# A transformer-layer kernel on one core: second phi matrix and gather issued after the first, odd work tied behind a pass's splits, row copies tied to the FFN's weight slabs

## The chip, the cores and the metric

The kernel runs on one core of a Trainium2 chip. The metric is device microseconds (us) of one execution, the median of three runs. Engines in the text: PE is TensorE (matmuls; PEld is its weight load), DVE is VectorE, ACT is ScalarE, POOL is GpSimd, SP is SyncE, which issues most DMAs here. Each engine runs its instructions in the order in which they were placed on it.

## The reference

One decoder layer over 512 prompt tokens and 32 sample tokens (8 sequences of 4), width 1024, FFN width 2816, all fp32:

- `mod = silu(c) @ w_ada + b_ada` gives shifts, scales and gates; `h = rmsnorm(x, norm1) * (1 + sc1) + sh1`.
- `h @ w_in` feeds a gated width-3 convolution and a native sparse attention: compressed blocks, selected blocks, a sliding window, each with its own keys and values. The compressed keys and values are `gelu(blocks @ w_phi1 + bias) @ w_phi2`, separately for K and V; for the sample tokens the blocks come from a paged cache through a page table, and the bias is the block position embedding `pe_cmp` times `w_phi1`.
- The two mixers are merged by sigmoid gates, projected by `w_out`, and added to x.
- `x += g2 * ((silu(h2 @ w_gate) * (h2 @ w_up)) @ w_down)`, then a last RMSNorm.
- Among the outputs is `new_win_sample = concat(cache_win, new rows)[:, 4:]`: the old window shifted by four rows.

## The kernel before

**Number format.** Every fp32 operand is split into a high and a low part. `split` (line 170) does this for a 128-column piece of a weight slab: ACT copies the piece into `wh` (L176), DVE subtracts into `wl` (L177); both tags have two buffers. `mm3` makes three matmuls of each product, in this order: wh with x high (L181), wh with x low (L182), wl with x high (L183). `to_hilo` (L211 on ACT, L212 on DVE) does the same for activations. Tokens come in two halves of 288 and 256 columns. A weight slab (`slab`, L167) is one 1 MB DMA on SP into one of three `raw` buffers.

**The start.** Before the projections a loop of 16 passes, n = 0 to 15, compresses the paged cache. A pass gathers 1 MB of rows (`cmp_gather`, L428, an indirect DMA issued by POOL, two `gt` buffers), copies them into transposable form (`cmp_copy`, L436, two DVE copies), transposes them (`cmp_T`: 16 transposes on PE, L444, four to a PSUM bank; ACT makes `xh`, L446; DVE makes `xl`, L447), and multiplies by the phi matrices (`cmp_M`: 24 matmuls a pass, 12 for K and 12 for V, L458 to L460). The two phi matrices are loaded by `phi_load` (L391, 1 MB each, `rphi`, into two of the three `raw` buffers) and split in quarters by `phi_split` (L396 on ACT, L397 on DVE). The third `raw` buffer holds the rows of c, of x_sample and of the convolution state (`xs`).

Between the passes lies odd work that uses the same engines: silu of c and its transposes (L549 to L553), `phi_bias` (`pb`, L403: 32 matmuls, the last readers of `rphi`), `x_rows` (transposes of x and its squares, L512 to L520), `mod_slab` (one slab of `w_ada`, L229, 16 instructions that the trace counts in 32 pieces), `inv_from_sums` and `inv_bcast` (the inverse norms, L255 to L294), `modulate`. The first slab of w_ada goes into the buffer of the first phi matrix, so it can only be issued when the first bias group has read that.

**The FFN.** Loop c2 = 1 to 10 (line 1343) loads one slab of w_gate and one of w_up (256 columns each) and takes them in two 128-column pieces. For a piece: split of the gate piece, its matmuls for both halves with `silu` on ACT into `ffg` (L1295), split of the up piece, its matmuls for both halves, and per half a DVE product `ffg` = up x silu (L1300), then f_hi on ACT (L211) and f_lo on DVE (L212). Eight 1016 KB copies from DRAM to DRAM make the shifted rows (`win_shift`, L1336).

**What sets the order.** The program is written in the order of its calls, but the framework's scheduler, with a cost model, places the instructions on each engine; `tc.issue_after(ins)` keeps what is written under it behind `ins`. A program order on an engine is fixed once it is built: an instruction whose input is late holds all that stand behind it on its engine.

Of the kernel before, what the change touches and what calls it, by code (L numbers as in the profile page):

```python
# [19 lines left out]
KC = 8  # L20
# [79 lines left out]
def build(tc, a, o):  # L100
# [19 lines left out]
    def tp_ps(nm):  # L120
        return ps.tile([128, 512], F32, tag="g", bufs=5, name=nm)
# [194 lines left out]
    def make_A(nT, sc, A):  # L316
        dve.tensor_scalar_add(A, sc, 1.0)
        dve.tensor_mul(A, A, nT.rearrange("p (k x) -> p k x", x=1).broadcast_to([128, 8, 9]))
# [70 lines left out]
    def phi_load(v):  # L389
        rw = raw_tile("rphi").rearrange("p (k f) -> p k f", k=16)  # L390
        sync.dma_start(rw, a["w_phi1"][v].rearrange("(k p) f -> p k f", p=128))  # L391
        rws.append(rw)

    def phi_split(v, qt):
        qv = lambda t: t.rearrange("p (s c) f -> p s c f", s=2)[:, :, 2 * qt:2 * qt + 2, :]
        act.activation(qv(wph[v]), qv(rws[v]), AF.Copy)  # L396
        dve.tensor_sub(qv(wpl[v]), qv(rws[v]), qv(wph[v]).bitcast(F32))  # L397

    def phi_bias(v):
        p = tp_ps(nm("pb"))  # L400
        for k in range(16):
            j = k % 4
            pe.matmul(p[32 * j:32 * j + 32, 0:128], lhsT=peT[:, v * 16 + k:v * 16 + k + 32], rhs=rws[v][:, k, :], start=(k < 4), stop=(k >= 12))  # L403
        t = wphip.tile([128, 128], F32, tag="pbs", bufs=2, name=nm("pbs"))
        dve.tensor_copy(t, p[:, 0:128])
        q = tp_ps(nm("pbt"))
        pe.matmul(q[:, 0:1], lhsT=t, rhs=sel, start=True, stop=True)
        dve.tensor_copy(pbias[:, v:v + 1], q[:, 0:1])
# [16 lines left out]
    def cmp_gather(bp, qt):  # L425
        t = gat.tile([128, 4 * 512], F32, tag="gt", bufs=2, name=nm("gt"))
        col = bp * 4 + qt
        pool.indirect_dma_start(out=t, out_offset=None, in_=ccv, in_offset=bass.IndirectOffsetOnAxis(ap=ixc[:, col:col + 1], axis=0))  # L428
        return t
# [10 lines left out]
    def cmp_T(v, g2t):  # L440
        for lp in range(2):
            p = tp_ps(nm("xt"))
            for g in range(4):
                pe.transpose(p[:, g * 128:(g + 1) * 128], g2t[lp][:, v * 4 + g].rearrange("p l d -> p (l d)"), ident)  # L444
            xo = xhb[v][:, lp * 512:lp * 512 + 512]
            act.activation(xo, p, AF.Copy)  # L446
            dve.tensor_sub(xlb[v][:, lp * 512:lp * 512 + 512], p, xo.bitcast(F32))  # L447

    def cmp_M(v, qt, po):
        for lp in range(2):  # L450
# [23 lines left out]
                    pe.matmul(p[0:63, b2 * 256 + g * 64:b2 * 256 + g * 64 + 64], lhsT=h1[:, (g * 2 + b2) * 63:(g * 2 + b2) * 63 + 63], rhs=w2[:, 1, :], start=True, stop=True)  # L474
            evac(vext[0:63, 2 * bp:2 * bp + 2, :], p[0:63, 0:512].rearrange("p (b x) -> p b x", b=2))

    pool.memset(vext[32:64], 0.0)

    xst = ExitStack()
    xp = mkpool(xst, "xp", side="right")  # L480
    xT = xbig("xT")
# [1 line left out]
    dve.memset(ss1, 1.0)  # L483
    phi_load(0)
    gts = [cmp_gather(0, 0)]
    sync.dma_start(xr[0], a["x_prompt"][0:128, :])
    phi_load(1)
    gts.append(cmp_gather(0, 1))
    sync.dma_start(crow[0:1], a["c_prompt"])
    sync.dma_start(crow[1:9], a["c_sample"])  # L490
    sync.dma_start(perow, a["pe_cmp"].rearrange("v l d -> (v l d)").rearrange("(k p) -> k p", p=128))
    sync.dma_start(w2, a["w_phi2"].rearrange("v p d -> p v d"))
    for r0, nme, n in ((24, "b_ada", 48), (0, "norm1", 8), (8, "norm2", 8), (16, "norm_f", 8), (72, "b_conv", 8), (80, "w_conv", 24)):
        s = a[nme]
        s = s.rearrange("a b -> (a b)") if len(s.shape) == 2 else s
        sync.dma_start(vrow[r0:r0 + n, :], s.rearrange("(k p) -> k p", p=128))
    sync.dma_start(xs, a["x_sample"])
    sync.dma_start(strow, a["state_conv"])
    for j in range(1, 4):
        sync.dma_start(xr[j], a["x_prompt"][j * 128:(j + 1) * 128, :])  # L500

    dve.tensor_reduce(sel, ident.rearrange("p (a b) -> p b a", b=32)[:, 0, :], axis=AX.X, op=ALU.add)
# [18 lines left out]

    wake()
    phi_split(0, 0)
    phi_split(1, 0)
    accs = {}

    def cmp_step(bp, qt, v):
        if qt == 0:
# [6 lines left out]
    for n in range(16):  # L535
        bp, qt = n // 4, n % 4
        g2t = cmp_copy(gts[n])
        if n + 2 < 16:
            gts.append(cmp_gather((n + 2) // 4, (n + 2) % 4))
        for v in range(2):  # L540
            cmp_T(v, g2t)
            if pend is not None:
                cmp_step(*pend)
            pend = (bp, qt, v)
        if n < 3:
            for v in range(2):
                phi_split(v, n + 1)
        if n == 0:
            act.activation(crow, crow, AF.Silu)  # L549
            cp = tp_ps("cp")  # L550
            for k in range(KC):
                pe.transpose(cp[:, k * 16:k * 16 + 9], crow[:, k * 128:(k + 1) * 128], ident[64:73, 64:73])
            dve.tensor_copy(cT[:, :, 0:9], cp[:, 0:128].rearrange("p (k n) -> p k n", k=8)[:, :, 0:9])  # L553
            pp = tp_ps("pep")
            pe.transpose(pp[:, 0:32], perow, ident[0:32, 0:32])
            dve.tensor_copy(peT[:, 0:32], pp[:, 0:32])
            for v in range(2):
                phi_bias(v)
            vp = tp_ps("vp")
            pe.transpose(vp[:, 0:104], vrow, ident[0:104, 0:104])  # L560
            dve.tensor_copy(vec, vp[:, 0:104])
        if n == 1:
            p = tp_ps("stp")
            for k in range(KC):
                pe.transpose(p[:, k * 16:(k + 1) * 16], strow[:, k * 128:(k + 1) * 128], ident[32:48, 32:48])
            dve.tensor_copy(stT, p[:, 0:128].rearrange("p (k n) -> p k n", k=8))
            x_rows(4)
        if n < 8:
            mod_slab(n)
        if 2 <= n < 6:  # L570
            x_rows(n - 2)
        if n == 6:
            iv = inv_from_sums(ss1, xp)
            iv2 = xp.tile([128, 3], F32, name="iv2")
            dve.tensor_copy(iv2[:, 0:2], iv[:, 0:2])
            dve.tensor_copy(iv2[:, 2:3], iv[:, 4:5])
            invs = (inv_bcast(iv2, 0, xp), inv_bcast(iv[:, 2:4], 1, xp))
        if n == 8:
            modp.pop()()
            make_A(n1T, sc1, A1)  # L580
            mods = [modulate(xT, invs[hf], A1, sh1, hh_, hl_, hf, xp) for hf in range(2)]
        if 8 <= n < 12:
            for g_ in mods:
                for _ in range(2):
                    next(g_)
        if n == 12:
            with tc.issue_after(last_slab[0].ins):
                sync.dma_start(x_dr, xT.rearrange("p k n -> p (k n)"))
            xst.close()
# [753 lines left out]
    for c2 in range(1, FC // 2):  # L1343
        sg, su = slab(a["w_gate"], c2 * 256), slab(a["w_up"], c2 * 256)
        if c2 <= DEC_B:
            win_shift(c2 - 1)
        for cc in range(2):
            c, g_ = c2 * 2 + cc, ffg()
            for v, fn in ((sg, lambda w, hf: ffn_gate(g_, w, hf)), (su, lambda w, hf: ffn_up(c, g_, w, hf))):
                w = split(v[:, :, cc * 128:cc * 128 + 128])  # L1350
                for hf in range(2):
                    fn(w, hf)
# [104 lines left out]
```

## Time and profile before

| | |
|---|---|
| median of 3 runs | 1346.72 us (1346.35 to 1346.86) |
| the profiled execution, its own time | 1346.54 us |
| its span in the trace | 1344.5 us |
| PE busy | 1311.2 us, 98% |
| DVE, ACT busy | 654.1 us (49%), 539.4 us (40%) |
| DMA | 193.56 MB, mean 144 GB/s |

How to read it: PE is busy nearly always, so idle time of PE is what there is to win, and new idle time of PE is what there is to lose. The time of the execution is 2.0 us above the span of the trace.

### The profile page before, as it was taken

To read this page: it belongs to the slowest core of one execution; us is meant where nothing else is said; L and a number is where in the kernel's file an instruction comes from. 1 tells how busy PE (TensorE), PEld (TensorE's weight loads), DVE (VectorE), ACT (ScalarE), POOL (GpSimd) and SP (SyncE) were. 2 spreads that over 40 slices of the span, in tenths; PEclk is the share of its full clock that TensorE was granted. 3 is DMA by queue.
4 is the path that set the end of the run, shared out by engine and by line. 5 is a ranking of instruction groups with operands and counts; after the bars stand their busy time and mean duration, and the time that the engine had idled before them with its cause. 6 is when DMAs were issued, how large, how long until landed. Compare 5 with 4: busy or idle time off the path is not lost.

```text
span 1344.5 us, 25740 instructions
## 1 busy us (share of the span) xinstructions
PE 1311.2 (98%) x10884; PEld 1212.8 (90%) x10884; DVE 654.1 (49%) x1570; ACT 539.4 (40%) x1065; POOL 69.3 (5%) x123
## 2 busy tenths in 40 slices
PE   5899999999999999999999999999999999999997
PEld 4778899999999999899777777999999999999996
DVE  3458623234454554425677676667433333323335
ACT  5335423433332334324676766435323223222223
POOL 2000030000111110001000000000000000000000
PEclk7999999999999999999999999999999999999998
DMA  7877225684534562664357246531112223123221
GB/s 263 314 275 291 95 78 175 221 266 141 206 126 170 189 236 98 168 158 130 111 163 201 90 120 167 162 128 63 64 64 95 95 64 125 56 87 87 87 63 67
DMA packets 138024, 193.56 MB, mean 144 GB/s; under 512 B 4817, under 2 KB 124761, under 8 KB 132918
## 3 DMA queue, kind: packets, MB, share of 16 engines
q1 hardware_dynamic: 133302, 149.98, 36.2%
q0 software_dynamic: 4608, 41.95, 8.4%
q8 instruction: 85, 1.39, 0.4%
q14 instruction: 29, 0.24, 0.0%
HBM read 174.47 MB, written 25.76 MB: 149 GB/s over the span
## 4 chain that ended last, share of the span: by engine, by line
PE 95%; DMA 2%; DVE 1%; ACT 0%; issue 0%; SPq 0%; POOL 0%; ACTq 0%; DVEq 0%; POOLq 0%
PE lin L181 19%; PE lin L182 19%; PE lin L183 19%; PE dn L181 3%; PE dn L182 3%; PE dn L183 3%; PE acc L1143 3%; PE ptp L1149 3%; PE xt L444 2%; PE phi L460 2%; PE phi L458 2%; PE phi L459 2%; PE modp L229 2%; PE kt L860 2%; PE sp L1118 1%; DMA rphi<-in_w_phi 1%
## 5 line engine op out<-in xcount | busy, mean ns | idle before, releaser
L181 PE MATMUL lin<-h_hi,wh 128*128 128x288 f32 (+1 forms) x1648 | 478.5, 291 | 0.0
L182 PE MATMUL lin<-h_lo,wh 128*128 128x288 f32 (+1 forms) x1648 | 474.5, 288 | 0.0
L183 PE MATMUL lin<-h_hi,wl 128*128 128x288 f32 (+1 forms) x1648 | 473.1, 287 | 0.0
L181 PEld LDWEIGHTS lin<-h_hi,wh 128*128 128x128 f32 x1648 | 310.5, 188 | 9.4 <-issue 8.1
L182 PEld LDWEIGHTS lin<-h_lo,wh 128*128 128x128 f32 x1648 | 310.0, 188 | 0.5
L183 PEld LDWEIGHTS lin<-h_hi,wl 128*128 128x128 f32 x1648 | 309.4, 188 | 0.3
L177 DVE TENSOR_TENSOR wl<-raw,wh 128x1024 fp32r<-128x1024 f32 x132 | 159.1, 1206 | 238.7 <-ACT wh L176 238.4
L176 ACT ACTIVATE wh<-raw 128x1024 fp32r<-128x1024 f32 x132 | 138.2, 1047 | 301.6 <-PE lin L182 204.0
L181 PE MATMUL dn<-f_hi,wh 128*128 128x256 f32 (+1 forms) x352 | 101.9, 290 | 0.0
L182 PE MATMUL dn<-f_lo,wh 128*128 128x256 f32 (+1 forms) x352 | 101.3, 288 | 0.0
L183 PE MATMUL dn<-f_hi,wl 128*128 128x256 f32 (+1 forms) x352 | 101.0, 287 | 0.0
L1125 ACT ACTIVATE P<-P,nms 128x512 f32<-128x512 f32 (+3 forms) x128 | 70.9, 557 | 18.7 <-DVE nms L1124 17.9
L1124 DVE CUSTOM_DVE_ANT_0 P<-sp,ta 128x512 f32<-128x512 f32 (+3 forms) x128 | 57.7, 483 | 31.0 <-PE sp L1112 23.5
L183 PEld LDWEIGHTS dn<-f_hi,wl 128*128 128x128 f32 x352 | 66.3, 188 | 0.0
L181 PEld LDWEIGHTS dn<-f_hi,wh 128*128 128x128 f32 x352 | 66.2, 188 | 0.0
L182 PEld LDWEIGHTS dn<-f_lo,wh 128*128 128x128 f32 x352 | 66.1, 188 | 0.0
L458 PE MATMUL phi<-xh,wph 128*128 128x512 f32 x128 | 53.5, 418 | 0.0
L459 PE MATMUL phi<-xh,wpl 128*128 128x512 f32 x128 | 51.4, 402 | 0.0
L460 PE MATMUL phi<-xl,wph 128*128 128x512 f32 x128 | 51.2, 400 | 0.0
L447 DVE TENSOR_TENSOR xl<-xt,xh 128x512 fp32r<-128x512 f32 x64 | 41.7, 687 | 19.0 <-ACT xh L446 19.0
L444 PE MATMUL xt<-ident,gt 128*128 128x128 f32 x256 | 36.6, 292 | 13.7 <-DVE gt L436 13.7
L446 ACT ACTIVATE xh<-xt 128x512 fp32r<-128x512 f32 x64 | 35.3, 598 | 33.8 <-PE xt L444 33.6
(372 smaller groups left out, 2119.8 us busy)
## 6 DMA issues: line engine op xcount, KB each, us to landing
raw<-in_w_in SPq DMA_DIRECT2D x26, 1024.0 KB, 8.6
raw<-in_w_ada SPq DMA_DIRECT2D x24, 1024.0 KB, 6.7
raw<-in_w_gate SPq DMA_DIRECT2D x11, 1024.0 KB
raw<-in_w_up SPq DMA_DIRECT2D x11, 1024.0 KB, 5.1
wraw<-in_cache_win POOLq DMA_DIRECT2D x8, 1024.0 KB, 7.0
raw<-in_w_down SPq DMA_DIRECT2D x8, 1024.0 KB, 5.7
out_new_win_sample<-in_cache_win SPq DMA_DIRECT2D x8, 1016.0 KB
rq<-in_w_in SPq DMA_DIRECT2D x8, 512.0 KB, 8.0
```

The costliest lines, as they stand in the source:

```text
L176: act.activation(oh, view, AF.Copy)
L177: dve.tensor_sub(ol, view, oh.bitcast(F32))
L181: pe.matmul(p, lhsT=wh[:, k, :], rhs=xh, start=start, stop=False)
L182: pe.matmul(p, lhsT=wh[:, k, :], rhs=xl, start=False, stop=False)
L183: pe.matmul(p, lhsT=wl[:, k, :], rhs=xh, start=False, stop=stop)
L444: pe.transpose(p[:, g * 128:(g + 1) * 128], g2t[lp][:, v * 4 + g].rearrange("p l d -> p (l d)"), ident)
L447: dve.tensor_sub(xlb[v][:, lp * 512:lp * 512 + 512], p, xo.bitcast(F32))
L458: pe.matmul(po, lhsT=w_h, rhs=mh, start=first, stop=False)
L459: pe.matmul(po, lhsT=w_l, rhs=mh, start=False, stop=False)
L460: pe.matmul(po, lhsT=w_h, rhs=ml, start=False, stop=last)
L1124: dve.tensor_tensor_reduce(out=t[:, 0:n], in0=sps[br], in1=t_dist[:, 512 - n:512], scale=-hs, scalar=3e38, op0=ALU.add, op1=ALU.min, accum ...
L1125: act.activation(t[:, 0:n], t[:, 0:n], AF.Exp, scale=-1.0, bias=nms[:, c:c + 1], accum_out=sums[:, c:c + 1])
```

## The change

Three things change.

1. The second phi matrix's load and the second gather are issued after four small loads (c, pe_cmp, w_phi2), and the load of the first 128 rows of x goes to the end with the other rows. The memset of `vext` moves on POOL from before the first gather to between the first and the second. The split of the second matrix's first quarter is written into pass 0, after its first transposes.
2. The odd work of a pass is put under `issue_after` of the last `xh` and the last `xl` of that pass, and most of it goes one pass later.
3. Each `win_shift` is put under `issue_after` of the FFN slab loaded just before it.

```diff
@@ cmp_T
-            act.activation(xo, p, AF.Copy)
-            dve.tensor_sub(xlb[v][:, lp * 512:lp * 512 + 512], p, xo.bitcast(F32))
+            last_x[0] = act.activation(xo, p, AF.Copy)
+            last_x[1] = dve.tensor_sub(xlb[v][:, lp * 512:lp * 512 + 512], p, xo.bitcast(F32))
...
-    pool.memset(vext[32:64], 0.0)
...
     gts = [cmp_gather(0, 0)]
-    sync.dma_start(xr[0], a["x_prompt"][0:128, :])
-    phi_load(1)
-    gts.append(cmp_gather(0, 1))
+    pool.memset(vext[32:64], 0.0)
     sync.dma_start(crow[0:1], a["c_prompt"])
     sync.dma_start(crow[1:9], a["c_sample"])
     sync.dma_start(perow, ...)
     sync.dma_start(w2, ...)
+    phi_load(1)
+    gts.append(cmp_gather(0, 1))
...
-    for j in range(1, 4):
+    for j in range(4):
         sync.dma_start(xr[j], a["x_prompt"][j * 128:(j + 1) * 128, :])
...
     phi_split(0, 0)
-    phi_split(1, 0)
     accs = {}
+    last_x = [None, None]
...
+        if n == 0:
+            phi_split(1, 0)
         if n < 3:
             for v in range(2):
                 phi_split(v, n + 1)
-        if n == 0:
-            (silu of c, cp, pep, phi_bias(0), phi_bias(1), vp)
-        if n == 1:
-            (stp, x_rows(4))
-        if n < 8:
-            mod_slab(n)
-        if 2 <= n < 6:
-            x_rows(n - 2)
-        if n == 6:
-            (inverse norms)
-        if n == 8:
-            (make_A, start of modulate)
-        if 8 <= n < 12:
-            (modulate)
+        with tc.issue_after(last_x[0].ins), tc.issue_after(last_x[1].ins):
+            if n == 0:
+                (pep, vp)
+            if n == 1:
+                (silu of c, cp, stp, phi_bias(0), phi_bias(1))
+            if n == 2:
+                x_rows(4)
+            if 1 <= n < 9:
+                mod_slab(n - 1)
+            if 3 <= n < 7:
+                x_rows(n - 3)
+            if n == 7:
+                (inverse norms)
+            if n == 9:
+                (make_A, start of modulate)
+            if 9 <= n < 13:
+                (modulate)
...
         if c2 <= DEC_B:
-            win_shift(c2 - 1)
+            with tc.issue_after(last_slab[0].ins):
+                win_shift(c2 - 1)
```

(Lines in round brackets stand for the calls that they name.)

How the order changes, at three places. **First place**, DVE at the start, from the last of the small index work: `wpl_156` and `wpl_157` are the low parts of the first and the second phi matrix, `gt_6`, `gt_7` the two copies of the first gather, `xl` the low parts of the transposed rows. Before:

```order
L502 TENSOR_REDUCE sel<-ident 128x1
L397 TENSOR_TENSOR wpl_156<-rphi_181,wph_154 128x2x256 x4
L397 TENSOR_TENSOR wpl_157<-rphi_186,wph_155 128x2x256 x4
L436 COPY gt_6_256<-gt_183 128x1024
L436 COPY gt_7_258<-gt_183 128x1024
L447 TENSOR_TENSOR xl_168<-xt_262,xh_166 128x512
```

And of the change, on the same engine at the same place:

```order
L500 TENSOR_REDUCE sel<-ident 128x1
L397 TENSOR_TENSOR wpl_156<-rphi_180,wph_154 128x2x256 x4
L436 COPY gt_6_254<-gt_182 128x1024
L436 COPY gt_7_256<-gt_182 128x1024
L397 TENSOR_TENSOR wpl_157<-rphi_189,wph_155 128x2x256 x4
L447 TENSOR_TENSOR xl_168<-xt_260,xh_166 128x512
```

The copies of the first gather now stand ahead of the second matrix's split instead of behind it. On ACT the four high parts of the second matrix still stand ahead of the first `xh`, and the silu of c (L549 before, L557 now) has gone from between them to behind the eight `xh` of the first two passes.

**Second place**, ACT in the FFN where one pair of slabs ends and the next begins (raw_11788 and raw_11790 are the next gate and up slabs; lin_11676 and lin_11702 are the last gate results of the pair before, 288 and 256 columns; `f_hi_10742` is the high part of the last up results). Before:

```order
L1295 ACTIVATE ffg_11671<-lin_11676 128x288
L176 ACTIVATE wh_11794<-raw_11788 128x1024
L1295 ACTIVATE ffg_11671<-lin_11702 128x256
L211 ACTIVATE f_hi_10742<-ffg_11671 128x288
L176 ACTIVATE wh_11850<-raw_11790 128x1024
L211 ACTIVATE f_hi_10742<-ffg_11671 128x256
L1295 ACTIVATE ffg_11793<-lin_11798 128x288
```

And of the change, on the same engine at the same place:

```order
L1297 ACTIVATE ffg_11671<-lin_11676 128x288
L1297 ACTIVATE ffg_11671<-lin_11702 128x256
L211 ACTIVATE f_hi_10742<-ffg_11671 128x288
L211 ACTIVATE f_hi_10742<-ffg_11671 128x256
L176 ACTIVATE wh_11794<-raw_11788 128x1024
L176 ACTIVATE wh_11850<-raw_11790 128x1024
L1297 ACTIVATE ffg_11793<-lin_11798 128x288
```

The high part of the next gate piece (`wh_11794`) has moved from between the two silus to behind both silus and both f_hi. On DVE its low part has moved in the same way, from before both products to behind the last f_lo: before `wl_11795` stood ahead of the product with lin_11732; now it stands behind `f_lo_10743` of 256 columns. It moves like this at six of the loop's boundaries (into c2 = 4 to 9) and stays as it was at the others.

**Third place**, PE at the same boundary (lin_11760 is the last up result, lin_11798 and lin_11824 the next gate results of 288 and 256 columns). Before:

```order
L183 MATMUL lin_11760<-h_hi,wl_11729 128x256
L181 MATMUL lin_11798<-h_hi,wh_11794 128x288
L182 MATMUL lin_11798<-h_lo,wh_11794 128x288
L183 MATMUL lin_11798<-h_hi,wl_11795 128x288
L181 MATMUL lin_11798<-h_hi,wh_11794 128x288
```

And of the change, on the same engine at the same place:

```order
L183 MATMUL lin_11760<-h_hi,wl_11729 128x256
L181 MATMUL lin_11798<-h_hi,wh_11794 128x288
L182 MATMUL lin_11798<-h_lo,wh_11794 128x288
L181 MATMUL lin_11824<-h_hi,wh_11794 128x256
L182 MATMUL lin_11824<-h_lo,wh_11794 128x256
L183 MATMUL lin_11798<-h_hi,wl_11795 128x288
```

The first two products of the second half now stand ahead of the first one that needs `wl`. Apart from the start and these six boundaries PE's order differs by two rows only. On SP, the eight row copies stand between the slabs of w_ada and w_in before, and each right behind an up slab of the FFN now.

## Rows read from the trace of the kernel before

**Rows 1.** The first page of the profile: busy time, share of the span and instructions of each engine.

```profile
PE 1311.2 (98%) x10884; PEld 1212.8 (90%) x10884; DVE 654.1 (49%) x1570; ACT 539.4 (40%) x1065; POOL 69.3 (5%) x123
```

**Rows 2.** The waits of PE, whole span: line and what it waited for, us in total, times, longest.

```profile
PE xt L444 <- DVE gt L436: 13.7, 1, 13.7
PE modp L229 <- DMA raw<-in_w_ada: 3.5, 1, 3.5
...
PE sacc L910 <- ACT pts L140: 1.0, 1, 1.0
PE ot L932 <- ACT ob L929: 0.8, 1, 0.8
```

**Rows 3.** The timeline of the first 33 us: start, duration, engine, line, operation, tiles, count, and in brackets the idle time of the engine before it and what ended that.

```profile
1.83 0.85 SPq L391 DMA_DIRECT2D rphi<-in_w_phi  x1
1.86 1.80 POOL L477 MEMSET vext<- 32x2048 f32 x1
2.73 1.91 SPq L486 DMA_DIRECT2D xr<-in_x_prompt  x1
...
4.85 0.72 SPq L391 DMA_DIRECT2D rphi<-in_w_phi  x1
...
5.14 1.16 POOL L428 DMA_INDIRECT gt<-in_cache_cmp,ixc  x1 [1.48 <-DVE ixc L369]
...
18.46 2.19 ACT L396 ACTIVATE wph<-rphi 128x512 fp32r<-128x512 f32 x4 [7.96 <-DMA rphi<-in_w_phi]
...
19.12 2.50 DVE L397 TENSOR_TENSOR wpl<-rphi,wph 128x512 fp32r<-128x512 f32 x4 [7.65 <-ACT wph L396]
...
20.67 1.28 ACT L549 ACT_TABLE_LOAD   x1
21.53 1.29 DVE L436 COPY gt<-gt 128x1024 f32<-128x1024 f32 x2
21.96 1.06 ACT L549 ACTIVATE xs<-xs 9x1024 f32<-9x1024 f32 x1
...
22.28 3.67 PE L444 MATMUL xt<-ident,gt 128*128 128x128 f32 x16 [13.66 <-DVE gt L436]
...
23.43 0.60 ACT L446 ACTIVATE xh<-xt 128x512 fp32r<-128x512 f32 x1 [0.41 <-PE xt L444]
...
25.60 0.78 PE L458 MATMUL phi<-xh,wph 128*128 128x512 f32 x1
...
30.42 1.08 PE L403 MATMUL pb<-rphi,peT 128*32 128x128 f32 x32
```

**Rows 4.** DMA queues between 10.0 and 14.1 us (packets, MB, share of 16 engines in that time: the first queue carries the gathers, the second SP's transfers), and the first gather's us from issue to landing, from the window around its issue.

```profile
q0 software_dynamic: 154, 1.16, 77.1%
q1 hardware_dynamic: 185, 0.38, 26.7%
...
gt<-in_cache_cmp,ixc POOLq DMA_INDIRECT x1, 9.5
```

**Rows 5.** The timeline at the first slab of w_ada, and from the first page the us from issue to landing (median) of 1 MB slabs in two stages.

```profile
31.56 2.40 SPq L167 DMA_DIRECT2D raw<-in_w_ada  x2
...
38.89 1.08 PE L229 MATMUL modp<-raw,cT 128*32 128x128 f32 x32 [3.47 <-DMA raw<-in_w_ada]
...
raw<-in_w_ada SPq DMA_DIRECT2D x24, 1024.0 KB, 6.7
...
raw<-in_w_up SPq DMA_DIRECT2D x11, 1024.0 KB, 5.1
```

**Rows 6.** Three windows of 5 us: busy us (and count) of PE, PEld, DVE, ACT, POOL, then the granted clock as a share of full speed, the DMA share and GB/s. The first holds the wait of 3.47 us, the second follows it, the third holds the two waits of 1.0 and 0.8 us.

```profile
35.00:40.00 5.00, 1.53 (x35) 0.95 (x34) 2.12 (x14) 0.21 (x1) 0.00 (x0) 1.00 1.34 473
40.00:45.00 5.00, 5.00 (x23) 4.69 (x24) 2.88 (x5) 2.67 (x5) 0.00 (x0) 0.66 0.67 228
540.00:545.00 5.00, 3.20 (x57) 2.58 (x57) 2.32 (x5) 4.47 (x7) 0.00 (x0) 1.00 0.17 51
```

**Rows 7.** Two pieces of the chain that ended last, in a later pass: start, us, what.

```profile
82.80 0.88 PE xt L444 x8
83.68 0.24 PE phi L458
```

**Rows 8.** The timeline at one boundary of the FFN loop: the split of the next gate piece (1045.16) and of the next up piece (1051.21, 1052.31), the first matmul of the next gate piece (1051.08), and the last product and its f_hi.

```profile
1045.16 1.06 ACT L176 ACTIVATE wh<-raw 128x1024 fp32r<-128x1024 f32 x1 [2.31 <-PE lin L182]
...
1051.08 0.30 PE L181 MATMUL lin<-h_hi,wh 128*128 128x288 f32 x1
...
1051.21 1.06 ACT L176 ACTIVATE wh<-raw 128x1024 fp32r<-128x1024 f32 x1 [1.84 <-PE lin L182]
...
1051.28 0.42 DVE L1300 TENSOR_TENSOR ffg<-lin,ffg 128x256 f32<-128x256 f32 x1 [1.42 <-PE lin L183]
...
1052.18 0.40 ACT L211 ACTIVATE f_hi<-ffg 128x256 fp32r<-128x256 f32 x1
...
1052.31 1.23 DVE L177 TENSOR_TENSOR wl<-raw,wh 128x1024 fp32r<-128x1024 f32 x1 [0.60 <-ACT wh L176]
```

**Rows 9.** SP's issue of the up slab whose first piece is split at 1051.21 (rows 8).

```profile
1035.43 0.37 SPq L167 DMA_DIRECT2D raw<-in_w_up  x1
```

**Rows 10.** The first and the last row of DVE's chain for the inverse norms, between them ten small instructions.

```profile
35.35 0.19 DVE L258 RECIPROCAL rmy<-rmy 128x5 f32<-128x5 f32 x1 [0.28 <-ACT rmy L257]
...
36.98 0.63 DVE L291 TENSOR_SCALAR dg<-ident,iv 128x128 f32<-128x128 f32 x3
```

More of the change, by code (lines that the diff above doesn't have):

```diff
@@ L547, in build @@
                 phi_split(v, n + 1)
-        if n == 0:
[L549 to L561, printed above, removed]
@@ L562, in build @@
-        if n == 1:
[L563 to L567, printed above, removed]
-        if n < 8:
-            mod_slab(n)
-        if 2 <= n < 6:
-            x_rows(n - 2)
-        if n == 6:
[L573 to L577, printed above, removed]
@@ L578, in build @@
-        if n == 8:
-            modp.pop()()
-            make_A(n1T, sc1, A1)
-            mods = [modulate(xT, invs[hf], A1, sh1, hh_, hl_, hf, xp) for hf in range(2)]
-        if 8 <= n < 12:
[L583 to L586, printed above, removed]
+        with tc.issue_after(last_x[0].ins), tc.issue_after(last_x[1].ins):
+            if n == 0:
+                pp = tp_ps("pep")
+                pe.transpose(pp[:, 0:32], perow, ident[0:32, 0:32])
+                dve.tensor_copy(peT[:, 0:32], pp[:, 0:32])
+                vp = tp_ps("vp")
+                pe.transpose(vp[:, 0:104], vrow, ident[0:104, 0:104])
+                dve.tensor_copy(vec, vp[:, 0:104])
+            if n == 1:
+                act.activation(crow, crow, AF.Silu)
+                cp = tp_ps("cp")
+                for k in range(KC):
+                    pe.transpose(cp[:, k * 16:k * 16 + 9], crow[:, k * 128:(k + 1) * 128], ident[64:73, 64:73])
+                dve.tensor_copy(cT[:, :, 0:9], cp[:, 0:128].rearrange("p (k n) -> p k n", k=8)[:, :, 0:9])
+                p = tp_ps("stp")
+                for k in range(KC):
+                    pe.transpose(p[:, k * 16:(k + 1) * 16], strow[:, k * 128:(k + 1) * 128], ident[32:48, 32:48])
+                dve.tensor_copy(stT, p[:, 0:128].rearrange("p (k n) -> p k n", k=8))
+                for v in range(2):
+                    phi_bias(v)
+            if n == 2:
[5 more added lines that the diff above has]
+            if n == 7:
+                iv = inv_from_sums(ss1, xp)
+                iv2 = xp.tile([128, 3], F32, name="iv2")
+                dve.tensor_copy(iv2[:, 0:2], iv[:, 0:2])
+                dve.tensor_copy(iv2[:, 2:3], iv[:, 4:5])
+                invs = (inv_bcast(iv2, 0, xp), inv_bcast(iv[:, 2:4], 1, xp))
+            if n == 9:
+                modp.pop()()
+                make_A(n1T, sc1, A1)
+                mods = [modulate(xT, invs[hf], A1, sh1, hh_, hl_, hf, xp) for hf in range(2)]
+            if 9 <= n < 13:
+                for g_ in mods:
+                    for _ in range(2):
+                        next(g_)
@@ L587, in build @@
+        if n == 13:
             with tc.issue_after(last_slab[0].ins):
```

## The prediction

> **What bounds the kernel now.** I read the busy times first: PE 98% of the span, no other engine above half [rows 1]. So a microsecond of PE idle time taken away is a microsecond won, and one added is one lost. The list of PE's waits says where idle time is: 13.7 us before the first transposes, 3.5 before the first slab of w_ada; two of 1.0 and 0.8 serve below as a measure [rows 2]. Third the timeline of the start, to see what those two waits are made of [rows 3 to 5]; fourth the FFN loop, where PE waits for nothing [rows 8], and to which the third part of the change takes its copies.
>
> The wait of 13.66 us looks like a wait for the gather, but the chain under it is another. The first gather was issued at 5.14 and landed 9.5 us later, at 14.6 [rows 3, 4]. Its copies start only at 21.53, because DVE has the low parts of the second phi matrix ahead of them, and that matrix landed at 18.46 [rows 3]. The first phi matmul starts at 25.60.
>
> **The start: both inputs sooner.** The copies of the gather now stand ahead of the second matrix's split. One of the two takes half of 1.29, so 14.6 + 0.65 gives transposes at 15.3; from the first transpose to the first phi matmul it was 25.60 − 22.28 = 3.32, so the data are there at 18.6. The other input is ACT: the first `xh` stands behind the four high parts of the second matrix. When does that land? Bytes that go ahead of it: before, half a MB of x rows, and both gathers beside it; now the first gather, and only part of the second, which is issued 1.8 us later, behind the memset [rows 3]. Between 10.0 and 14.1 the queues moved 1.16 + 0.38 MB in 4.1 us, 0.376 MB/us [rows 4]. Without 1.57 MB (x rows and one gather) it would land 4.2 sooner, at 14.3; with nothing gained, at 18.46. I take 15.5, nearer the first, since part of the second gather stays. (The four small loads ahead of it on SP may hold its issue back; the bound without any gain covers that.) Then 2.19 of high parts and 0.60 for an `xh` give 18.3 [rows 3], within the 18.6. DVE's low parts end 0.66 + 2.50 after the landing, at 18.7, one `xl` of 0.69 follows, and the third row of PE's new order wants the third `xh` at about 19.3: about 0.5 of new waiting there. So the start gives 25.60 − 18.6 − 0.5 = 6.5, **−6.5 us**; bounds −3.8 (matrix at 18.46: 18.46 + 2.19 + 0.60 = 21.3, and the 0.5) and −9.5 (no small waits, matrix at 14.3, and the gather 2.5 sooner too, since the x rows are out of its way as well).
>
> Against this stands a rule. The Trainium skill, "DMA: Bandwidth & Descriptors", section "Issuing engines are not separate DMA queues", says that transfers issued by different engines end up on the same 16 DMA engines and interleave. The trace agrees: a gather issued by POOL and SP's transfers moved side by side, 1.16 and 0.38 MB in the same 4.1 us [rows 4]. By it the second matrix need land no sooner, and the sum would be 1365.3 instead of 1362.6; that is the second rival below.
>
> **The odd work: one wait for two.** Before, between the first phi matmul and the first slab of w_ada PE waited 3.47 for the slab [rows 2, 5]. It can be issued when the first bias group has read the buffer: that began at 30.42, the issue was at 31.56 [rows 3, 5]. Of the change PE has, between that group and the slab, twelve phi matmuls of 0.24 [rows 7], the second group of 1.08 and two small reductions of some 0.3: 4.5 us. The slab lands in 6.7 (median of its stage), so PE waits 2.2; with the 5.1 of the FFN's slabs 0.6, with the 7.2 seen at this place 2.7 [rows 5]. The silu, with its table load 1.28 + 1.06 [rows 3], now stands behind the `xh` of two passes; its transposes follow twelve phi matmuls (2.9 us), less what the `xh` ahead of the silu take: wait 0.6, bounds 0 and 1.5. Together 2.8 for 3.47: **−0.7**, bounds −2.9 and +0.7.
>
> The clock: in the 5 us after the 3.47 wait the granted clock averaged 0.66 against 1.00 ahead of it [rows 6]. The lower level (1.2 of 2.4 GHz) therefore held for (1 − 0.66) × 5 × 2 = 3.4 us, and it cost half of that, 1.7. The two waits of 1.0 and 0.8 close together cost none: clock 1.00 [rows 6]. A wait of 2.2 lies between; I take half back, **−0.9** (0 to −1.7).
>
> The inverse norms: before, DVE's chain ran from 35.35 to 37.6 in the shadow of the wait for the slab [rows 5, 10]. Now it is tied behind pass 7's splits; with a table load (1.28) and the square root ahead it takes some 4 us, against one pass's phi matmuls of 12 × 0.24 = 2.9 and a few transposes of 0.88 [rows 7]: 0 to +1.5, I take **+0.7**. The rest of the odd work comes a pass later with all inputs long there, at nothing; passes have 12 × 0.24 of matmuls after each transposing [rows 7] to cover it.
>
> **The row copies themselves: nothing.** Early, PE has no wait for DMA but the one above [rows 2], so taking 1 MB copies away there gives nothing. In the FFN the up slab is issued at 1035.43 and its first piece split at about 1051.2 before the change, 15.8 us later, of which it needs 5.1 [rows 5, 8, 9]. A copy of the same size beside it costs another 5.1 at most, and is hidden. Behind each copy on SP stands the next gate slab, which waits for a buffer anyway and is early by as much; the copy's end is waited for by nobody before the end of the program.
>
> **What the tie moves: the splits at the boundaries.** This decides. At six of the loop's boundaries the next gate piece's high part now stands on ACT behind both f_hi, and its low part on DVE behind the last f_lo. Before the change PE passes from the last up matmul to the next gate matmul at 1051.08 without a gap, since the gate's `wh` had been made at 1045.16, during the up piece [rows 8]. After it, from the row times: the product of the second half starts at 1051.28, 0.20 after PE's last up matmul, and ends at 1051.70. f_hi starts 0.04 later (as `wl` at 1052.31 behind `wh`, which ends at 1052.27) and ends, 0.40 long, at 1052.14. `wh` may start 0.09 ahead of that (as f_hi at 1052.18 ahead of 1052.27), and ends, 1.06 long, at 1053.11; PE goes on at 1053.16, a wait of **2.08**. Four matmuls are there that need only `wh`: 1088 columns at the phi matmuls' 0.24 for 512 [rows 7], 0.51, to 1053.67. The fifth needs `wl`, 1.23 long and started at 1053.15: ready for PE at 1054.43, a wait of **0.76**. Sum 2.84 at a boundary, × 6 = **+17.0 us**. PE is saturated on both sides, so nothing gives it back. Bounds: 2.08 alone, if `wl` came at once, 12.5; and 2.84 with 0.3 of extra latency at each of two steps, 20.6.
>
> What two waits of 2.08 and 0.76, half a microsecond apart, do to the clock lies between rows. Waits of 1.80 together cost nothing, one of 3.47 cost 1.7 [rows 2, 6]. (2.84 − 1.80)/(3.47 − 1.80) = 0.62, so I count 3.7 of six boundaries at 1.7: **+6.3**, bounds 0 and 10.2.
>
> **Sum.** 1346.54 (the profiled execution, 2.0 above its span of 1344.5) − 6.5 − 0.7 − 0.9 + 0.7 + 17.0 + 6.3 = 1362.4; the median of the runs lies 0.2 above the profiled one: **1362.6**, 1.2% slower.
>
> **The rivals.** *No clock loss at the boundaries*: the two waits are split by matmuls and each is below 2.1, nearer the 1.80 than the 3.47. Then 1362.6 − 6.3 = 1356.3, with the start's bounds 1353 to 1359. Chance 0.20. *The second matrix lands no sooner* (18.46, phi at 21.3 and the small waits as before): start −3.8 for −6.5, 1365.3. For it speaks that the queues share; against it that half a MB is out of the way. Chance 0.08. *The other side: ACT and DVE do not hold the split back.* If the next gate piece's `wh` is ready by PE's last up matmul in spite of its new place, the boundary is as seamless as at 1051.08 [rows 8], and only the start is left: 1362.6 − 23.3 = 1339.3, range 1335 to 1342. It decides at 7.4/6 = 1.2 us of waiting at a boundary: below that the kernel gets faster. Against it: the product of the second half reads a result that PE finishes with its last up matmul, so the chain 0.42 + 0.40 + 1.06 cannot start earlier. Chance 0.07. *About half of it*: waits of 1.2 at a boundary, or three boundaries instead of six, and the time stays where it is, 1346 ± 2.7. Chance 0.04.
>
> **How the numbers follow.** The forecast has 0.61: six boundaries with two to six clock losses, 1357 to 1368. A change within 0.2%, 2.7 us, counts as none, about what a measurement of this kernel can tell. Slower takes the forecast and the first two rivals: 0.89. Faster 0.07, same 0.04. The range reaches down over the rival without clock loss, to 1352, and up over the late matrix with all six losses, 1362.6 + 2.7 + 3.9, to 1369; it leaves out the two cases below and little above.
>
> **What would show it.** PE's list of waits: L181 for `wh` (ACT), six times about 2.1, and L183 for `wl` (DVE), six times about 0.8. The granted clock below 1.00 in windows behind some boundaries. At the start the wait before the first transposes shrunk from 13.66 to about 6.7, the first phi matmul at 18 to 19, and a wait of about 2 for the first w_ada slab. The prediction is wrong if the FFN's waits are not there, if they are a different number than six, or if the start's gain is eaten by the second matrix.

## The result and the profile after

The changed kernel takes 1359.08 us (median of four runs, 1358.43 to 1361.15) against 1346.65 before: ratio 1.0095, 95% interval 1.0078 to 1.0113. The profiled execution took 1358.56 us, with a span of 1356.7.

The same places of the two traces, by the start of PE's first instruction there:

| place | before | after | shift |
|---|---|---|---|
| first transposes of the first pass | 22.28 | 13.05 | −9.23 |
| first phi matmul | 25.60 | 21.02 | −4.58 |
| first matmul of the projections | 175.56 | 169.79 | −5.77 |
| first matmul of the FFN | 936.12 | 929.91 | −6.21 |
| first matmul of the down projection | 1196.20 | 1208.44 | +12.24 |
| last transposes of the output | 1335.25 | 1347.50 | +12.25 |

So the start won 6.2 us, and the FFN loop lost 18.45. PE's waits of the changed kernel (line, what it waited for, us in total, times, longest) name both; they answer to [rows 2]:

```profile
PE lin L181 <- ACT wh L176: 11.5, 6, 1.9
PE xt L444 <- DVE gt L436: 5.0, 1, 5.0
PE phi L458 <- ACT xh L446: 4.3, 1, 4.3
PE lin L183 <- DVE wl L177: 2.4, 5, 0.5
...
PE modp L229 <- DMA raw<-in_w_ada: 0.8, 1, 0.8
...
PE ib L293 <- DVE dg L291: 0.7, 1, 0.7
...
PE cp L560 <- ACT xs L557: 0.3, 1, 0.3
```

The first and the fourth row are new and lie in the FFN. The wait of 13.7 before the first transposes has become two, 5.0 before them and 4.3 behind them.

**One boundary of the FFN**, timeline (start, duration, engine, line, tiles, and in brackets the idle time of the engine and what ended it), answering to [rows 8]:

```profile
1047.67 0.28 PE L183 MATMUL lin<-h_hi,wl 128*128 128x256 f32 x1
1047.99 0.42 DVE L1302 TENSOR_TENSOR ffg<-lin,ffg 128x256 f32<-128x256 f32 x1 [1.35 <-PE lin L183]
1048.44 0.42 ACT L211 ACTIVATE f_hi<-ffg 128x256 fp32r<-128x256 f32 x1 [2.30 <-DVE ffg L1302]
1048.77 1.99 ACT L176 ACTIVATE wh<-raw 128x1024 fp32r<-128x1024 f32 x2
1048.89 0.43 DVE L212 TENSOR_TENSOR f_lo<-ffg,f_hi 128x256 fp32r<-128x256 f32 x1 [0.48 <-ACT f_hi L211]
1049.84 2.36 DVE L177 TENSOR_TENSOR wl<-raw,wh 128x1024 fp32r<-128x1024 f32 x2 [0.52 <-ACT wh L176]
1049.86 0.40 PE L181 MATMUL lin<-h_hi,wh 128*128 128x288 f32 x1 [1.91 <-ACT wh L176]
...
1051.12 0.40 PE L183 MATMUL lin<-h_hi,wl 128*128 128x288 f32 x1 [0.48 <-DVE wl L177]
1051.36 0.29 PE L181 MATMUL lin<-h_hi,wh 128*128 128x288 f32 x1
```

Read it down the chain: PE's last up matmul, the product, f_hi, the split, PE. Matmuls of 256 columns come every 0.12 us, so without a wait the next would have started at 1047.79; it starts at 1049.86, 2.07 later. The row for `wl` comes 1.26 after that, of which 0.51 are matmuls: 0.75. After each stall the second matmul comes 0.24 behind the first, where 0.13 is usual; at the first stall this lies inside the 0.75, at the second it is 0.1 more. From one boundary to the next PE took 27.10 us here (1049.86 to 1076.96), before 24.19 (1051.08 to 1075.27): 2.91 for each boundary.

**The clock at the boundaries**: windows of 5 us (PE busy, count, granted clock, DMA share, GB/s). Five of the six look like the first row; at one the clock fell.

```profile
1101.00:1106.00 5.00, 2.60 (x19) 1.00 0.00 0
1129.00:1134.00 5.00, 3.09 (x13) 0.72 0.00 0
1134.00:1139.00 5.00, 5.00 (x39) 0.94 0.01 3
```

The first row of the three belongs to a boundary with the clock at full rate, the other two to the one at 1131.16. From that one to the next the distance was 28.07 (1131.16 to 1159.23), 0.97 more than elsewhere. The lower clock held for (1 − 0.72) × 5 × 2 + (1 − 0.94) × 5 × 2 = 3.4 us and cost half of that, 1.7; from this goes the wait for `wl`, 0.75, which does not occur there. Sum: 5 × 2.91 + 3.88 = 18.4, the 18.45 of the table. The DMA share is 0: no copy and no slab is under way at the boundaries.

**The start**, timeline, answering to [rows 3]:

```profile
5.14 1.16 POOL L428 DMA_INDIRECT gt<-in_cache_cmp,ixc  x1 [3.34 <-DVE ixc L369]
...
5.51 0.74 SPq L391 DMA_DIRECT2D rphi<-in_w_phi  x1
...
8.30 0.97 POOL L428 DMA_INDIRECT gt<-in_cache_cmp,ixc  x1 [0.16 <-issue]
...
12.30 1.29 DVE L436 COPY gt<-gt 128x1024 f32<-128x1024 f32 x2 [0.64 <-DMA gt<-in_cache_cmp,ixc]
13.05 3.68 PE L444 MATMUL xt<-ident,gt 128*128 128x128 f32 x16 [4.97 <-DVE gt L436]
...
18.29 2.19 ACT L396 ACTIVATE wph<-rphi 128x512 fp32r<-128x512 f32 x4 [7.60 <-DMA rphi<-in_w_phi]
...
20.39 2.04 ACT L446 ACTIVATE xh<-xt 128x512 fp32r<-128x512 f32 x4
21.02 0.79 PE L458 MATMUL phi<-xh,wph 128*128 128x512 f32 x1 [4.29 <-ACT xh L446]
```

The gather is copied at 12.30, 9.2 us sooner. But the second matrix is there at 18.29, where it was 18.46 before, and ACT has it ahead of the first `xh`. So PE has its transposes done at 16.7 and waits 4.3. The windows show what that wait costs besides (same columns as above, for all engines PE, PEld, DVE, ACT, POOL):

```profile
13.00:18.00 5.00, 3.68 (x16) 3.28 (x16) 0.60 (x1) 0.00 (x0) 1.46 (x2) 0.50 1.06 345
18.00:21.00 3.00, 0.00 (x0) 0.00 (x0) 2.05 (x4) 2.71 (x6) 0.00 (x0) 0.50 1.00 333
21.00:26.00 5.00, 4.99 (x13) 3.55 (x14) 3.54 (x7) 1.42 (x3) 0.00 (x0) 0.57 1.01 379
26.00:31.00 5.00, 5.00 (x32) 4.13 (x31) 3.19 (x6) 1.54 (x3) 1.15 (x1) 1.00 0.33 78
```

The phi matmuls from 21.0 on run at 0.57 on average, at half rate for (1 − 0.57) × 5 × 2 = 4.3 us, which costs 2.15. Before, the low clock had mostly fallen on transposes and on only some 0.7 us of phi matmuls.

### The profile page after: what moved, and what is told of

It is laid out like the page before. It is cut to its first block, busy times and chain, and to the rows that moved or that the text cites. A ratio compares the mean times of both kernels' runs of the same rounds, so it can differ in the third digit from the quotient of the medians.

```text
span 1356.7 us, 25742 instructions
## 1 busy us (share of the span) xinstructions
PE 1315.6 (97%) x10884; PEld 1213.6 (89%) x10884; DVE 653.4 (48%) x1570; ACT 538.8 (40%) x1066; POOL 69.5 (5%) x123
## 4 chain that ended last, share of the span: by engine, by line
PE 94%; DVE 2%; ACT 1%; DMA 1%; issue 1%; SPq 0%; POOL 0%; ACTq 0%; POOLq 0%; DVEq 0%
PE lin L181 19%; PE lin L183 19%; PE lin L182 19%; PE dn L181 3%; PE dn L182 3%; PE dn L183 3%; PE acc L1145 3%; PE ptp L1151 3%; PE phi L458 2%; PE phi L460 2%; PE phi L459 2%; PE xt L444 2%; PE modp L229 2%; PE kt L862 2%; PE sp L1120 1%; PE sp L1121 1%
## 5 line engine op out<-in xcount | busy, mean ns | idle before, releaser
L181 PE MATMUL lin<-h_hi,wh 128*128 128x288 f32 (+1 forms) x1648 | 479.6, 291 | 11.5 <-ACT wh L176 11.5
L1127 ACT ACTIVATE P<-P,nms 128x512 f32<-128x512 f32 (+3 forms) x128 | 70.6, 555 | 18.8 <-DVE nms L1126 18.1
L1302 DVE TENSOR_TENSOR ffg<-lin,ffg 128x288 f32<-128x288 f32 (+1 forms) x44 | 19.4, 441 | 84.0 <-PE lin L183 84.0
L447 DVE TENSOR_TENSOR xl<-xt,xh 128x512 fp32r<-128x512 f32 x64 | 41.2, 684 | 17.1 <-ACT xh L446 16.9
```

The source lines that it names most:

```text
L181: pe.matmul(p, lhsT=wh[:, k, :], rhs=xh, start=start, stop=False)
L447: last_x[1] = dve.tensor_sub(xlb[v][:, lp * 512:lp * 512 + 512], p, xo.bitcast(F32))
L1127: act.activation(t[:, 0:n], t[:, 0:n], AF.Exp, scale=-1.0, bias=nms[:, c:c + 1], accum_out=sums[:, c:c + 1])
```

## The experiments

**1 to 4: is it the order, or the copies?** The theory: the tie (the `issue_after` on the row copies) made the scheduler move the splits, and this order alone costs the 18.45. The rival: the copies' traffic in the FFN.

Run `untied`, the change without its third part:

```diff
-            with tc.issue_after(last_slab[0].ins):
-                win_shift(c2 - 1)
+            win_shift(c2 - 1)
```

> The changed kernel with its first two parts, and the row copies written as before (no tie). Theory (the loss is the order of the splits at six FFN boundaries, which the tie brought): the boundaries are seamless again, PE's list of waits has no L181 for wh in the FFN, and the time is 1346.65 - 6.2 = 1340.4 us. Rival (the loss is the clock or the start): the waits may go, but the time stays above 1346.65.

Measured 1350.94 us, ratio to before 1.0034 (1.0021 to 1.0046): 10.5 us above the theory, and in the range of the rival. In the FFN the theory held: PE has no wait there, and from its first matmul (+4.10 us against before) to the down projection (+4.11) nothing is lost. But a new wait stands among the projections, and it follows SP's rows, not the order of the FFN's splits:

```profile
PE lin L181 <- ACT wh L176: 7.7, 1, 7.7
```

```profile
250.90 16.56 SPq L632 DMA_DIRECT2D out_new_win_prompt<-stage  x2
267.51 0.50 SPq L636 DMA_DIRECT2D v_dr<-stage  x1
268.06 0.91 SPq L642 DMA_DIRECT2D out_new_win_sample<-rows  x1
...
271.62 0.45 SPq L708 DMA_DIRECT2D rq<-in_w_in  x1
276.71 0.32 SPq L726 DMA_DIRECT2D q_dr0h<-qh  x1
277.23 0.32 SPq L726 DMA_DIRECT2D q_dr0l<-ql  x1
277.60 6.75 SPq L708 DMA_DIRECT2D rq<-in_w_in  x5
```

```profile
282.76 2.00 ACT L176 ACTIVATE wh<-rq 128x1024 fp32r<-128x1024 f32 x2 [6.07 <-DMA rq<-in_w_in]
```

(The first fence is PE's waits, the second SP's timeline, the third ACT's.) The q weights come in eight loads, two to a buffer. The split at 282.76, for which PE waits, needs the third and the fourth. The third, at 271.62, stands on SP behind stores whose data come only from 267 on. The fourth is the first of the five at 277.60; it stands behind two stores of q results, which go out only at 276.71 and 277.23. In the changed kernel the last six of these loads went out between 245.75 and 268.2, ahead of the stores of q results. PE waits 7.69, until 283.87. Behind that the granted clock is 0.50 from 280 to 285, where PE works for 1.13 us, and 0.63 from 285 to 290: some 4.8 us of work at half rate, which cost 2.4. Together this is 10.1 of the 10.2 us by which this trace falls back between the projections (−6.09) and the FFN (+4.10). So the tie also gave another order on SP at the projections, one without this wait; I had put this at nothing. That the place of the stores is the cause is read from these rows and was not tried by itself.

Run `tie_only`, the kernel before with the third part alone (the same two lines the other way round):

> The kernel before with the third part of the change alone (row copies tied to the slabs). Theory: six boundaries with waits of 1.9 and 0.5 us, 1346.65 + 18.5 = 1365.1 us, and nothing won at the start. Rival (parts one and two share in the loss): between 1347 and 1359 us.

Measured 1364.92 us, ratio 1.0134 (1.0117 to 1.0150). The FFN loses 18.5, with the waits of the changed kernel (11.5 in 6, 2.4 in 5). The theory holds to 0.2 us.

Run `order_only`, the kernel before, copies early, only the splits tied. `last_f` holds the last f_hi and f_lo; the lines that set it are left out at the dots.

```diff
...
-                w = split(v[:, :, cc * 128:cc * 128 + 128])
+                with ExitStack() as late:
+                    if 4 <= c2 <= 9 and cc == 0 and v is sg:
+                        for i in last_f:
+                            late.enter_context(tc.issue_after(i.ins))
+                    w = split(v[:, :, cc * 128:cc * 128 + 128])
```

> The kernel before, its row copies early as they were, SP's order the same; only the next gate piece's split is tied behind the last f_hi and f_lo at the boundaries into c2 = 4 to 9. PE's order at a boundary then has seven matmuls ahead of the first that needs wl, three of which need the up piece's wh. Theory (order alone): a wait of 2.08 for wh and of about 0.55 for the second wh, six times 2.6, and a clock loss or none: 1362 to 1364 us. Rival (the copies' DMA traffic beside the slabs makes the loss): 1346.65 us.

Measured 1364.28 us, ratio 1.0135 (1.0118 to 1.0153), 0.3 above the range. No row copy is near, and the loss is there: 17.9 us in the FFN. PE's list has 12.2 us in 10 waits for `wh`: six of 1.91, four short ones of 0.2 for the second `wh` (I had said 0.55). At the two boundaries without a short one the clock fell (0.72 and 0.68 in the windows of 5 us that hold them).

Run `kept`, copies tied as in the change, the split order restored: the split of each next gate piece is written ahead of the matmuls of the up piece before it, and that piece's matmuls, products and f_hi are tied behind it. The next pair's slabs and copy move ahead of them too; they are left out at the dots.

```diff
-                w = split(v[:, :, cc * 128:cc * 128 + 128])
+            w = nxt
+            for hf in range(2):
+                ffn_gate(g_, w, hf)
+            w = split(su[:, :, cc * 128:cc * 128 + 128])
+            if cc == 0:
+                nxt = split(sg[:, :, 128:256])
+            elif c2 + 1 < FC // 2:
...
+                nxt = split(sg[:, :, 0:128])
+            with tc.issue_after(last_split[0].ins), tc.issue_after(last_split[1].ins):
                 for hf in range(2):
-                    fn(w, hf)
+                    ffn_up(c, g_, w, hf)
```

> The changed kernel with the row copies tied to the FFN's slabs as there, but with the last up piece's products, f_hi and f_lo of each pair tied behind the next gate piece's split, so that wh stands ahead of the two f_hi again. Theory (order alone): no wait of L181 in the FFN, 1340.4 us, as without the tie. Rival (the copies' traffic): 1358 us as the changed kernel.

Measured 1340.55 us, ratio 0.9951 (0.9934 to 0.9968), faster than the kernel before and the changed one, and where the theory had it. One window over the FFN (us, PE busy, granted clock, DMA share, GB/s):

```profile
940.00:1190.00 250.00, 250.00 (x1991) 1.00 0.34 113
```

PE has no idle time, with seven of the eight copies in it (the first is issued at 925.75 and meets no new wait either). Order without copies loses 17.9, copies without the order lose nothing: the rival is out.

**5 and 6: which part carries the start?** From `kept`, one part undone each.

Run `start_kept` (odd work written as before):

> The variant with tied copies and kept split order (1340.55 us), with the second part of the change undone: odd work written as before, matrix and gather later as changed. Theory (both parts share in the start): the first phi matmul 4.6 us sooner than before, but 1.7 of it lost to the lower clock that now falls on phi matmuls, and the old wait for the first w_ada slab stays: -2.9 us, 1343.7. Rival (the matrix and gather carry the whole gain): 1340.6 us.

Measured 1346.2 us, ratio 0.9999 (0.9989 to 1.0008): a miss by 2.5 us. The first phi matmul comes 4.62 sooner, as said, but the projections start only 0.15 sooner. The wait for the first slab did not stay at 3.5; it grew:

```profile
PE phi L458 <- ACT xh L446: 4.6, 1, 4.6
PE modp L229 <- DMA raw<-in_w_ada: 4.3, 1, 4.3
PE xt L444 <- DVE gt L436: 3.9, 1, 3.9
```

The slab comes at 38.4, 0.5 sooner than before. Where the rest of the 4.62 goes can be read from PE: the same 24 phi matmuls and the odd work between them take 13.07 us up to this wait at a mean clock of 0.75 (20.98 to 34.05), where they took 9.81 at 0.96 before (25.60 to 35.41). That is 3.3 for slower work, mostly the low clock on the phi matmuls, where I had said 1.7 for the clock, and 0.9 for the longer wait.

Run `odd_kept` (matrix, gather and x rows issued as before):

> The same variant (1340.55 us) with the first part of the change undone: second matrix, gather and x rows issued as before, odd work tied and a pass later. Theory (both parts share): the first phi matmul at 25.6 as before, the wait for the first slab 3.5 shrinks to about 1 and its clock loss of 1.7 goes, a wait of 0.7 for the inverse norms comes: -3.4 us, 1343.2. Rival (the matrix and gather carry the whole gain): 1346.6 us.

Measured 1343.43 us, ratio 0.9977 (0.9968 to 0.9987), as said. The slab wait is 0.78, the wait of 0.67 for the inverse norms is there. The parts are not additive: to the start of the projections −0.15 and −2.37 alone, −5.30 together, and in the medians −0.4 and −3.2 alone, −6.0 together. PE's order suggests why, though no run takes it by itself: the odd work's later place puts a second pass ahead of the slab, so that the earlier phi matmuls do not run into its wait.

**7 and 8: who keeps the second matrix late?** Both on `kept`, with a small copy on POOL that reads the second matrix.

Run `late_third` (in the trace the copy stands behind the second gather and ahead of the third):

```diff
+    seen = gat.tile([128, 1], F32, name="seen")
+    pool.tensor_copy(seen, rws[1][:, 15, 127:128])
     gts.append(cmp_gather(0, 1))
```

> The same variant (1340.55 us); GpSimd reads one column of the second phi matrix before it issues the third gather, so that this gather starts only when the matrix has landed. Every other engine's order is the same. Theory (the third gather, issued at 13.9 now that the copies of the first run early, takes the matrix's share of the DMA engines): the matrix lands about 1.7 us sooner, at 16.6, and the first phi matmul at about 19.3. Rival (the matrix is late for another reason, its own issue or its queue): it lands at 18.3 as before and the time does not fall.

Measured 1339.84 us, ratio 0.9952 (0.9936 to 0.9969), within the runs of `kept`. The matrix's split starts at 17.88, against 17.83 in `kept`, though the third gather is issued at 18.73 instead of 14.06. My theory of the third gather falls.

Run `late_second` (the same read, written into the second gather's own buffer):

> As the run with the third gather held back, but the second gather is held back until the second phi matrix has landed (one element of its buffer is written from the matrix first), and the third stands behind it. Theory: the matrix lands at about 14.8, 3.5 us sooner, the first phi matmul at about 17.6; the second gather lands about 20 and is needed at about 21.6: 1340.55 - 3.4 = 1337 us. Rival (the matrix's own queue is the limit): 18.3 again, and the second gather, 6 us later, makes a new wait: 1342 to 1346 us.

```profile
15.76 2.19 ACT L396 ACTIVATE wph<-rphi 128x512 fp32r<-128x512 f32 x4 [5.10 <-DMA rphi<-in_w_phi]
...
16.54 1.43 POOL L430 DMA_INDIRECT gt<-in_cache_cmp,ixc  x1 [0.56 <-POOL gt L429]
18.28 1.45 POOL L430 DMA_INDIRECT gt<-in_cache_cmp,ixc  x1 [0.30 <-issue]
26.99 0.69 DVE L438 COPY gt<-gt 128x1024 f32<-128x1024 f32 x1 [5.57 <-DMA gt<-in_cache_cmp,ixc]
```

Measured 1342.72 us, ratio 0.9972 (0.9962 to 0.9983). The matrix comes at 15.76, 2.1 us sooner: since holding the third alone changed nothing, it is the second gather that takes its share. But that gather then lands at 27.0 with the third beside it, and PE waits 3.46 for its copy. Each theory had half: the mechanism of the one, the price of the other.

**9 and 10: towards a better version.** Run `split_after`: on `kept`, the second matrix's split goes behind the first pass's `xh` and `xl`, which need only the first matrix.

```diff
-        if n == 0:
-            phi_split(1, 0)
         if n < 3:
-            for v in range(2):
-                phi_split(v, n + 1)
+            phi_split(0, n + 1)
+        if n == 0:
+            with tc.issue_after(last_x[0].ins), tc.issue_after(last_x[1].ins):
+                for q in range(4):
+                    phi_split(1, q)
```

> The variant with tied copies and kept split order (1340.55 us); the second phi matrix's four quarter splits are tied behind the first pass's last xh and xl instead of standing ahead of the first xh. Theory (after the reorder the first phi matmul waits only because ACT holds the first xh behind that matrix's split): the first phi matmul follows the transposes at about 16.8 instead of 20.55, its twelve matmuls run at the lower clock while the matrix lands at 17.8: 1340.55 - 3.5 = 1337 us. Rival (the next inputs are late anyway: gathers, the slab of w_ada): the gain turns into later waits, above 1339.5 us.

Measured 1338.9 us (1335.5 to 1340.41), ratio 0.9935 (0.9918 to 0.9952), the fastest median here; its interval overlaps that of `kept`. In the profiled execution the wait behind the transposes is gone, and the first phi matmul comes at 18.1 (the first gather landed later in it, and the transposes started at 14.8). But the projections start only 0.1 sooner than in `kept`:

```profile
PE xt L444 <- DVE gt L436: 6.0, 1, 6.0
PE modp L229 <- DMA raw<-in_w_ada: 3.1, 1, 3.1
```

The wait for the slab is back, and behind it the granted clock is 0.72 from 41 to 46 us, where it is 1.00 in `kept`. In this trace, the slowest of the four runs, the rival is right; the median lies between.

Run `warm`. At the start PE makes 44 transposes whose result nobody reads (`wake`, L418); here, on `split_after`, there are 84.

> As the run with the splits tied behind the first pass, with 84 instead of 44 dummy transposes at the start, so that PE has work until about 12.8, just ahead of the first transposes. Theory (the lower clock at the start comes from PE's idle time and is paid in phi matmuls): the granted clock stays at 1.00 to 13 and for the transposes, and another 2 to 3 us go: 1334 to 1335 us. Rival (inputs bound the first passes, not the clock): within 0.7 us of the run without the dummies.

Measured 1343.27 us, ten runs from 1339.57 to 1349.04. Both the theory and the rival missed, by 8 us and by 4. In its trace the granted clock is 1.00 to 13 us, as meant. But the first gather is copied only at 15.20 (14.05 in `split_after`, 12.49 in `kept`), PE waits 2.6 for it, and the clock is 0.89 from 13 to 18 and 0.61 from 18 to 21, so that the first phi matmuls again meet the lower level. The projections start 0.5 sooner than in `split_after`, the FFN 0.5 later. So the run does not decide what the low clock at the start is worth; why the gather comes later and why the runs scatter so is open.

## Why the prediction came out

Forecast 1362.6, measured 1359.08; slower, as said, and by the step that was said to decide. But the time lies nearer to the first rival, 1356.3 without a clock loss, and came with one loss where the forecast had two to six. Term by term:

- **The boundaries, +17.0: right.** Six places, 2.08 and 0.76 forecast, 2.07 and 0.75 found at the boundary shown. With the slow start after each stall it is 2.91 a boundary instead of 2.84, 17.5 in all. `order_only` shows that the order suffices, `kept` that it is needed.
- **The clock there, +6.3: mis-sized.** It fell at one boundary of six and cost 0.97. This is 5.3 us too much, and more than the whole error of the forecast. I drew a line between 1.80 us of waiting (no loss) and 3.47 (1.7 lost). It was entered with 2.84, a distance between starts, while 1.80 and 3.47 are idle times: with the 2.39 of idle time found (1.91 and 0.48) it gives 2.1 boundaries and 3.6 us. And its upper end is not a fixed price. `order_only` has the start of the kernel before, and PE waits there for the same slab; the rows are of the kernel before, then of `order_only`:

```profile
39.90 3.62 PE L444 MATMUL xt<-ident,gt 128*128 128x128 f32 x16
```

```profile
38.86 1.08 PE L228 MATMUL modp<-raw,cT 128*32 128x128 f32 x32 [3.31 <-DMA raw<-in_w_ada]
39.88 1.97 PE L443 MATMUL xt<-ident,gt 128*128 128x128 f32 x16
```

  After 3.47 us of waiting the transposes took 3.62 us, after 3.31 in `order_only` 1.97, with the granted clock at 1.00 from 35 to 45. So one trace gave the line a point that another does not have. At the boundaries one of six fell in the changed kernel and in `tie_only`, two in `order_only`.
- **The first phi matmul, −6.5: −4.6.** The step that failed is the second matrix's landing: 15.5 forecast, 18.29 found. That was the second rival, which put the first phi matmul at 21.3; it came at 21.02, without the 0.5 of small waits behind it. (The bound of −9.5 does not follow from its own terms: a matrix at 14.3 would give the first `xh` at 17.1, and −8.5.) The room that the x rows left went to the gathers: the first was copied at 12.30, where it had landed at 14.6 before, and `late_second` shows that the second keeps the matrix back. The forecast took away the bytes ahead of the matrix and let the rest flow at one rate; how unevenly the queues shared stands in the last section. By the Trainium skill, "DMA: Bandwidth & Descriptors", section "Issuing engines are not separate DMA queues", transfers of different issuers interleave on the same 16 engines; these runs agree, 2.1 us for one gather.
- **A term that I had left out**: the low clock then falls on phi matmuls, 2.15 against some 0.4 before, +1.8.
- **Odd work: better than said.** The waits for silu and slab are 0.3 and 0.8, not 0.6 and 2.2: −2.4 for −0.7, and the clock loss of 1.7 behind the old wait is gone whole, −0.9 forecast; since it is gone in `order_only` too, with the wait still there, this much of the gain hangs on which trace stands for the kernel before. The inverse norms: +0.7 forecast, 0.67 found. Together −4.6 − 2.4 − 1.7 + 0.7 + 1.8 = −6.2 at the start of the projections, where −5.77 was measured; 0.4 is not accounted for, less than by what two traces of one start can differ (1.65 in `order_only`).
- **The copies, 0: right in the FFN** (`kept`), **wrong about the early part**. Another 0.4 is won among the q projections (−5.77 to −6.19), by what is not shown, and `untied` shows that with the new start and without the tie the order there costs 10.2.
- The start as a whole was forecast at −7.4 and gave −6.2; the errors in it largely cancelled, which was luck. In the whole sum 5.3 too much for the clock stands against 0.5 too little at the boundaries and 1.2 too much gain at the start: 3.6, the error of 3.5.

## What to carry to other kernels

A tie on a DMA is an input to the scheduler: read the order it yields on every engine, at places far from the edit too, before you price the edit itself. Where a split stands behind the results of the piece before it, its whole chain (product, high part, split) becomes PE idle time, and could be added up here from row durations to 0.02 us (2.08 and 2.07, 0.76 and 0.75). A clock loss read behind one wait of one trace is one draw: look for the same wait in other traces before it is made a price. Two waits that feed one matmul are not worth their sum: taking one away counts only as far as the next input is early.

## What the runs showed of the hardware

At the FFN boundaries PE stood for 1.91 us, worked for four matmuls and stood for 0.48; in the changed kernel's trace the granted clock stayed at 1.00 (2.4 GHz) at five and fell to the lower level (1.2 GHz) at one of six otherwise like places, two in `order_only`. So the same wait has no fixed price: 2.91 or 3.88 us. Nor has a longer one: before the first slab of w_ada PE stood for 3.47 us in the kernel before and the clock fell, and for 3.31 in `order_only` and it stayed at 1.00.

In an idle stretch of 4.97 us at the start the clock fell (0.77 on average from 10 to 13 us); it was at 0.50 for the transposes, stayed there through 3.7 us of work and 4.3 of waiting, and rose only in the phi matmuls from 21 us on.

While a gather and SP's loads moved together, their queues had about as many packets, but not as many bytes. The changed kernel from 9 to 10 us (packets, MB, share of 16 engines; the first queue carries the gathers, the second SP's transfers, the second matrix among them):

```profile
q0 software_dynamic: 40, 0.33, 83.0%
q1 hardware_dynamic: 36, 0.07, 19.2%
```

Per packet this is some 8 KB for the gather and 2 KB for the loads, so the loads had less than a fifth of the bytes; from 12 to 13 us, with the gathers nearly still, they had 137 packets and 0.28 MB. In `late_second` the second gather, issued at 16.54 instead of 8.3, took 10.4 us to land (9.0 in `kept`), but not by sharing alone: its queue moved nothing from the issue to 21 us, while SP's loads moved 348 GB/s from 18 to 21. Why it began so late is not shown.
